# Attention: the loads that stack K and Q are issued by GpSimd in place of SyncE

## The chip, the core and the metric

The kernel runs on one core of a Trainium2 chip. Its engines are TensorE (PE in the profile, its weight loads PEld), VectorE (DVE), ScalarE (ACT), GpSimd (POOL) and SyncE (SP), which here only issues transfers. The metric is the device time of one execution in microseconds (us); lower is better.

## The reference, cut to what matters

One step of a two-layer network over 128 context tokens and 1024 latent tokens (1152 together, `T` in the kernel). The first layer is a state-space mixer with pooling. The second, which this study is about, has 8 differential attention heads (two softmaxes over all keys, one subtracted from the other) and 16 windowed heads that share 4 key heads; the kernel works on them two at a time, in 8 window blocks.

```python
def diff_attention(q, k, v, lam):
    ...
        s = jnp.einsum('bhiqd,bhikd->bhiqk', qb, k).astype(jnp.float32) * scale
        p = jax.nn.softmax(s, axis=-1)
        attn = p[:, :, 0] - lam * p[:, :, 1]
        return jnp.einsum('bhqk,bhkv->bhqv', attn.astype(v.dtype), v)
...
def window_sink_attention(q, k, v, k_ctx, v_ctx, sink):
    ...
        s_w = jnp.einsum('bkgqd,bkwd->bkgqw', qb, kw).astype(jnp.float32) * scale
        s_w = jnp.where(valid, s_w, NEG_INF)
        s_c = jnp.einsum('bkgqd,bkld->bkgql', qb, k_ctx).astype(jnp.float32) * scale
        logits = jnp.concatenate([s_c, s_w, jnp.broadcast_to(sk, s_c.shape[:-1] + (1,))], axis=-1)
        p = jax.nn.softmax(logits, axis=-1).astype(v.dtype)
```

## The kernel before

Every float32 operand of a matmul is split into a float16 high part and a float16 remainder, and products are summed from the parts.

The second layer runs in two stages. The **differential stage** (lines 1473 to 1490) goes over 8 heads, numbered 0 to 7. The **window stage** (lines 1494 to 1509) goes over 8 pairs of window heads, numbered here 8 to 15 after the keys of their Q projections. Each head or pair goes over 9 query blocks of 128 rows, b = 0 to 8. For each block PE forms the scores S from Q and K (line 1288, in the window stage lines 1367 and 1370), DVE and ACT make the softmax, ACT writes the high part of the probabilities into the tile `phl` (line 1304 or 1389), POOL subtracts and writes the remainder (line 1305 or 1390, called the **split** below), SP transposes `phl` by a DMA into the tile `PT` (line 1233), and PE multiplies `PT` by V (line 1321 or 1407). That last product, called PV below, is put off: the PV of block b runs on PE three blocks later, so the PV of block 5 runs at the very end of a pair and those of blocks 6 to 8 in the next.

While a head is worked on, PE also makes the next head's projections, piece by piece between the score matmuls (the `Filler`). `qk_block` (line 1158) makes one K or Q: after the matmuls the result is rotated, with POOL doing the two last steps of each of three pieces (lines 1180 and 1181, on the tiles `sw` and `q`), then ACT writes the high half of `qhl` (line 1187) and POOL the remainder (line 1188). Four transfers then stack the halves of `qhl` from partitions 0 to 63 and 64 to 127 into the tile `K` or `Q` (lines 1193 and 1198): one for each of two matrices `m` and two halves `x`. There are 10 such K and 16 such Q, so 40 and 64 transfers, all issued by SP. The first S of a head or pair needs them all.

Engines take their instructions in order. PE's order is written out by hand (`manual_schedule`), those of the other engines come from a scheduler. SP issues all transfers of the attention in one queue: weights, transposes, K and Q loads, outputs. A transfer that still waits for its input holds up what stands behind it.

Of the kernel before, what the change touches and what calls it, by code (L numbers as in the profile page):

```python
# [22 lines left out]
T = TC + TL  # L23
# [197 lines left out]
class Builder:  # L221
# [936 lines left out]
    def qk_block(self, key, src, hs, cache=None, kout=None, scale=1.0, pre=None):  # L1158

        nc = self.nc  # L1160
        q = self.tl(self.rot, [P, TK], F32, "q32", 2)
        n = T if cache is None else TK
        if cache is not None:
            nc.sync.dma_start(q[:, T:TK], cache)

        def evac(ps, c0, c1):
            raw = self.tl(self.rot, [P, 384], F32, "raw", 2)
            o = TC if c0 == 0 else 0
            nc.scalar.activation(raw[:, o:], ps[:, o:], AF.Copy, scale=scale)
            if c0 == 0:  # L1170
                nc.scalar.activation(q[:, :TC], ps[:, :TC], AF.Copy, scale=IWS * scale)
            a, b = c0 + o - TC, c1 - TC

            if pre is None:
                nc.vector.scalar_tensor_tensor(q[:, c0 + o:c1], ps[:, o:], scale, self.cosT[:, a:b], ALU.mult, ALU.mult)  # L1175
            else:
                nc.vector.tensor_tensor(q[:, c0 + o:c1], raw[:, o:], self.cosT[:, a:b], ALU.mult)
            sw = self.tl(self.rot, [P, 384], F32, "sw", 2)
            nc.vector.stream_shuffle(sw[:, o:], raw[:, o:], [(i + 16) % 32 for i in range(32)])  # L1179
            nc.gpsimd.tensor_tensor(sw[:, o:], sw[:, o:], self.sinT[:, a:b], ALU.mult)  # L1180
            nc.gpsimd.tensor_tensor(q[:, c0 + o:c1], q[:, c0 + o:c1], sw[:, o:], ALU.add)

        yield from self.g_proj(src, hs, evac, pre)
        if kout is not None:
            nc.sync.dma_start(kout, q[:, :TC])
        hl = self.tl(self.rot, [P, 2, TK], F16, "qhl", 2)
        nc.scalar.activation(hl[:, 0, :n], q[:, :n], AF.Copy)
        nc.gpsimd.tensor_tensor(hl[:, 1, :n], q[:, :n], hl[:, 0, :n], ALU.subtract)
        if cache is not None:
            d = self.wt([P, 2, TK], F16, tag="K", bufs=2)  # L1190
            for m in range(2):
                for x in range(2):
                    nc.sync.dma_start(d[x * 64:x * 64 + 64, m], hl[m * 64:m * 64 + 64, x])
        else:
            d = self.wt([P, 2, 2, T], F16, tag="Q", bufs=2)
            for m in range(2):
                for x in range(2):
                    nc.sync.dma_start(d[x * 64:x * 64 + 64, m], hl[m * 64:m * 64 + 64, :, :T])
        self.R[key] = d

    def v_block(self, key, src, hs, vout):
# [450 lines left out]
```

## Time and profile before

| | us |
|---|---|
| median of 3 runs | 2256.24 (2253.14 to 2256.71) |
| the profiled execution, its time | 2259.94 |
| the profiled execution, its span from first to last instruction | 2258.0 |
| PE busy in the span | 2025.2 (90%) |
| DVE busy | 1470.4 (65%) |
| ACT busy | 1223.2 (54%) |
| POOL busy | 1060.9 (47%) |

The 1.9 us between the profiled execution's time and its span lie before the first and after the last instruction. The profile's page gives, for each group of instructions, the engine, the operation, the tile written and the tiles read, the number, the busy time and the idle time of the engine just before them with what ended it. The timeline has one row for each instruction: start in us from the span's start, duration in us, engine, line, operation, tiles, shapes, and in brackets the engine's idle time before it with the releaser. SPq rows are the issues of SP: their duration is that of the issue, not of the transfer. A busy share is an average over stages, so the rows below are taken from the stages in which the changed transfers stand.

### The profile page before, as it was taken

The page shows a single profiled execution, that of the slowest core. Times are in us where ns is not written, and L with a number is a line of the kernel's source. Part 1 is how long each engine was busy: PE and PEld are TensorE (multiplying, and loading weights), DVE is VectorE, ACT ScalarE, POOL GpSimd, SP SyncE. Part 2 cuts the span into 40 slices and gives each one's busy share as a digit, 9 for nine tenths or more (in the row PEclk, how much of TensorE's full clock was granted, in tenths as well). Part 3 has the DMA queues.
Part 4 walks back from the last instruction along what each step waited for, and adds up shares of the span by engine and source line. Part 5 has one row for each costly group of instructions (what it writes and reads, how often), then busy time and mean ns, then how long its engine had stood idle before and what let it go on. Part 6 is the DMA issues. An engine that isn't in the chain of part 4 may idle for free.

```text
span 2258.0 us, 49764 instructions
## 1 busy us (share of the span) xinstructions
PE 2025.2 (90%) x20258; PEld 1433.6 (63%) x20258; DVE 1470.4 (65%) x2722; ACT 1223.2 (54%) x2891; POOL 1060.9 (47%) x997
## 2 busy tenths in 40 slices
PE   5997788887989999998998999999988998998997
PEld 2654475564556655665776776776666777785566
DVE  5878988789586445575677677767765545451334
ACT  5575666566463312344655655665567867782321
POOL 1378677876675200044345345445446655661001
PEclk8998898998999999999999999999999999999999
DMA  7221513224557622035454554555456968899312
GB/s 281 72 79 48 152 58 102 75 94 122 183 202 217 164 99 88 31 132 118 95 122 108 117 123 113 112 126 115 109 123 134 175 146 160 163 176 210 139 47 84
DMA packets 435125, 283.10 MB, mean 125 GB/s; under 512 B 374448, under 2 KB 385232, under 8 KB 434896
## 3 DMA queue, kind: packets, MB, share of 16 engines
q1 hardware_dynamic: 433920, 279.34, 49.9%
q8 instruction: 158, 2.59, 0.5%
q10 hardware_dynamic: 976, 0.58, 0.1%
q14 instruction: 71, 0.58, 0.1%
HBM read 133.38 MB, written 29.05 MB: 72 GB/s over the span
## 4 chain that ended last, share of the span: by engine, by line
PE 42%; DVE 20%; POOL 10%; ACT 9%; issue 6%; DMA 5%; SPq 2%; POOLq 0%; ACTq 0%; DVEq 0%
PE psmm L329 8%; PE psmm L330 8%; PE psmm L331 8%; DVE sms L1290 3%; PE psS L1288 3%; DVE whl L323 3%; PE psm L329 2%; PE psm L330 2%; PE psm L331 2%; DVE p L1303 2%; DMA Q<-qhl 2%; ACT p L1380 1%; ACT p L1292 1%; DVE E L801 1%; PE psss L331 1%
## 5 line engine op out<-in xcount | busy, mean ns | idle before, releaser
L329 PE MATMUL psmm<-h,whl 128*128 128x384 f16 (+1 forms) x1104 | 370.2, 336 | 21.3 <-DVE q L1175 14.7
L330 PE MATMUL psmm<-h,whl 128*128 128x384 f16 (+1 forms) x1104 | 369.1, 335 | 2.3 <-DVE h L506 1.7
L331 PE MATMUL psmm<-h,whl 128*128 128x384 f16 (+1 forms) x1104 | 369.0, 335 | 0.0
L329 PE MATMUL psmm<-whl,h 128*128 128x128 f16 x1920 | 334.0, 220 | 10.1 <-DVE V L1211 10.1
L330 PE MATMUL psmm<-whl,h 128*128 128x128 f16 x1920 | 333.7, 220 | 0.0
L331 PE MATMUL psmm<-whl,h 128*128 128x128 f16 x1920 | 333.6, 220 | 0.0
L330 PEld LDWEIGHTS <-whl 128*128 128x128 f16 x2256 | 225.5, 100 | 167.9 <-issue 47.2
L331 PEld LDWEIGHTS <-whl 128*128 128x128 f16 x2256 | 225.2, 100 | 157.1 <-issue 18.9
L329 PEld LDWEIGHTS <-whl 128*128 128x128 f16 x2256 | 226.3, 100 | 147.3 <-issue 23.3
L1305 POOL TENSOR_TENSOR phl<-p,phl 128x1152 f16<-128x1152 f32 (+1 forms) x72 | 155.9, 2169 | 218.5 <-ACT phl L1304 218.5
L330 PEld LDWEIGHTS <-h 128*128 128x128 f16 x2520 | 246.7, 98 | 12.6 <-issue 10.8
L329 PEld LDWEIGHTS <-h 128*128 128x128 f16 x2520 | 246.8, 99 | 4.3 <-issue 2.6
L331 PEld LDWEIGHTS <-h 128*128 128x128 f16 x2520 | 246.6, 98 | 0.0
L323 DVE SCALAR_TENSOR_TENSOR whl<-w,whl 128x512 f16<-128x512 f32 x248 | 196.5, 811 | 67.0 <-ACT whl L322 66.0
L1290 DVE TENSOR_REDUCE sms<-psS 128x1 f32<-128x1152 f32 (+1 forms) x136 | 176.5, 1298 | 67.0 <-PE psS L1288 66.2
L1390 POOL TENSOR_TENSOR phl<-p,phl 128x1024 f16<-128x1024 f32 (+2 forms) x72 | 135.1, 1876 | 106.8 <-ACT phl L1389 85.8
L322 ACT ACTIVATE whl<-w 128x512 f16<-128x512 f32 x248 | 140.1, 609 | 78.2 <-PE psmm L331 42.2
L1288 PE MATMUL psS<-K,Q 128*128 128x512 f16 (+1 forms) x800 | 153.2, 328 | 25.1 <-DVE p L1303 19.3
L1180 POOL TENSOR_TENSOR sw<-sw,sin 128x384 f32<-128x384 f32 (+1 forms) x78 | 85.8, 1101 | 150.6 <-DVE sw L1179 127.2
L503 POOL TENSOR_TENSOR h<-mt,h 128x384 f16<-128x384 f32 (+2 forms) x32 | 28.9, 913 | 250.0 <-ACT h L502 250.0
L1288 PEld LDWEIGHTS <-Q 128*128 128x128 f16 x800 | 73.5, 99 | 94.2 <-DVE p L1303 21.9
L1292 ACT ACTIVATE psS<-psS,sms 128x1152 f32<-128x1152 f32 (+1 forms) x72 | 79.1, 1098 | 89.4 <-DVE sms L1290 88.9
(396 smaller groups left out, 5864.7 us busy)
## 6 DMA issues: line engine op xcount, KB each, us to landing
w<-in_wod SPq DMA_DIRECT2D x52, 512.0 KB, 4.0
w<-in_wev SPq DMA_DIRECT2D x40, 512.0 KB, 4.1
E<-csrow SPq DMA_DIRECT2D x36, 512.0 KB, 4.0
Q<-qhl SPq DMA_DIRECT2D x64, 288.0 KB, 4.3
go_dr<-gl SPq DMA_DIRECT2D x15, 576.0 KB, 3.9
wada<-in_w_ada SPq DMA_DIRECT2D x32, 256.0 KB, 5.8
o<-in_w_ada SPq DMA_DIRECT2D x16, 512.0 KB, 5.8
xT<-in_w_ada SPq DMA_DIRECT2D x16, 512.0 KB, 6.1
```

The source lines that it names most:

```text
L322: nc.scalar.activation(hl[:, 0, a:e], w[:, a:e], AF.Copy if scale is None else AF.Identity, scale=sc)
L323: nc.vector.scalar_tensor_tensor(hl[:, 1, a:e], w[:, a:e], sc, hl[:, 0, a:e], ALU.mult, ALU.subtract)
L329: mm(out, ah, bh, start=start, stop=False)
L330: mm(out, ah, bl, start=False, stop=False)
L331: mm(out, al, bh, start=False, stop=stop)
L1180: nc.gpsimd.tensor_tensor(sw[:, o:], sw[:, o:], self.sinT[:, a:b], ALU.mult)
L1288: nc.tensor.matmul(sv[:, i, c0:c1], q[:, m, x, qs], k[:, m, o + c0:o + c1], start=x == 0, stop=x == 1)
L1290: nc.vector.tensor_reduce(out=sm[:, ms[0]:ms[-1] + 1], in_=sv, axis=AX.X, op=ALU.max, negate=True)
L1292: nc.scalar.activation(sv[:, i] if m else e, sv[:, i], AF.Exp, bias=sm[:, m:m + 1], accum_out=sm[:, 4 + m:5 + m])
L1303: nc.vector.scalar_tensor_tensor(p[0], p[1], sm[:, 2:3], p[0], ALU.mult, ALU.add)
L1305: nc.gpsimd.tensor_tensor(phl[:, w:2 * w], p[0], phl[:, :w], ALU.subtract)
L1390: nc.gpsimd.tensor_tensor(phl[:, 2 * w:4 * w], p, phl[:, :2 * w], ALU.subtract)
```

## The change

The two `dma_start` calls that stack K and Q go from SP's queue to POOL's. Nothing else in the source changes: sizes, tiles and waits for data are the same.

```diff
@@ -1190,12 +1190,12 @@
             d = self.wt([P, 2, TK], F16, tag="K", bufs=2)
             for m in range(2):
                 for x in range(2):
-                    nc.sync.dma_start(d[x * 64:x * 64 + 64, m], hl[m * 64:m * 64 + 64, x])
+                    nc.gpsimd.dma_start(d[x * 64:x * 64 + 64, m], hl[m * 64:m * 64 + 64, x])
         else:
             d = self.wt([P, 2, 2, T], F16, tag="Q", bufs=2)
             for m in range(2):
                 for x in range(2):
-                    nc.sync.dma_start(d[x * 64:x * 64 + 64, m], hl[m * 64:m * 64 + 64, :, :T])
+                    nc.gpsimd.dma_start(d[x * 64:x * 64 + 64, m], hl[m * 64:m * 64 + 64, :, :T])
         self.R[key] = d
```

The orders of PE, DVE and ACT stay word for word the same. POOL's and SP's change. On POOL in the window stage, at the Q of the second pair (L1188 is the last step of Q's split, L1390 the splits of the probabilities of blocks 5 and 6):

```order
 L1390 TENSOR_TENSOR phl_21686<-p_21598,phl_21686 128x1024
 L1188 TENSOR_TENSOR qhl_21552<-q_2258_21263,qhl_21552 128x1152
+L1198 DMA Q_21555<-qhl_21552 64x2x1152 x4
 L1390 TENSOR_TENSOR phl_21789<-p_21692,phl_21789 128x1024
 L1390 TENSOR_TENSOR phl_21892<-p_21795,phl_21892 128x1024
```

All four loads now stand in one piece between the end of Q's split and the split of block 5. The same place on SP, where L1233 are the transposes of blocks 4, 5, 6 and 7 and L312 is a load of weights:

```order
 L312 DMA w_2470_23138<-in_wod 128x1024
 L1233 DMA_TRANSPOSE PT_21689<-phl_21686 128x16x128
-L1198 DMA Q_21555<-qhl_21552 64x2x1152 x2
 L1233 DMA_TRANSPOSE PT_21792<-phl_21789 128x16x128
-L1198 DMA Q_21555<-qhl_21552 64x2x1152
 L1233 DMA_TRANSPOSE PT_21895<-phl_21892 128x16x128
-L1198 DMA Q_21555<-qhl_21552 64x2x1152
 L1233 DMA_TRANSPOSE PT_21995<-phl_21992 128x16x128
```

The transposes now stand next to one another; before, the third and fourth load stood behind one and two of them. On POOL in the differential stage, at the K of head 2 (L1180 and L1181 rotate the first piece of the next Q, L1305 is a split of probabilities):

```order
 L1188 TENSOR_TENSOR qhl_13289<-q_1502_13053,qhl_13289 128x1280
+L1193 DMA K_13292<-qhl_13289 64x1280 x2
+L1180 TENSOR_TENSOR sw_13368<-sw_13368,sin_11482 128x256
+L1193 DMA K_13292<-qhl_13289 64x1280
+L1181 TENSOR_TENSOR q_1533_13297<-q_1533_13297,sw_13368 128x256
+L1193 DMA K_13292<-qhl_13289 64x1280
 L1305 TENSOR_TENSOR phl_13336<-p_13204,phl_13336 128x1152
-L1180 TENSOR_TENSOR sw_13368<-sw_13368,sin_11482 128x256
-L1181 TENSOR_TENSOR q_1533_13297<-q_1533_13297,sw_13368 128x256
```

Here the four K loads stand ahead of the split of probabilities, and the first piece's rotation has also gone ahead of it.

## The prediction

> **What bounds the kernel now.** I read the stages by window first, then what PE waits for in each, then the timeline of POOL, SP and PE where K and Q are loaded. Columns of the first view: the stretch, its length, busy time of PE, PEld, DVE, ACT and POOL with instructions, granted clock, DMA share, GB/s.
>
> ```profile
> 1025.00:1677.00 652.00, 601.01 (x6806) 457.38 (x6806) 467.66 (x697) 386.89 (x758) 301.92 (x185) 0.97 0.52 114
> 1677.00:2050.00 373.00, 332.99 (x4787) 272.11 (x4786) 192.68 (x596) 272.61 (x772) 221.41 (x138) 0.95 0.83 160
> ```
>
> The first row is the differential stage, the second the window stage. PE is the bound of both (601 of 652 us, 333 of 373 us), and POOL is busy 46% and 59% of the time. Whatever this change does, it does through PE's waits. From the view of waits (waiter, releaser, us in total, times, longest), the two rows on L1288 over the differential stage, the three others over the window stage:
>
> ```profile
> PE psS L1288 <- DVE p L1303: 19.3, 11, 5.1
> PE psS L1288 <- DMA Q<-qhl: 5.7, 2, 3.9
> ...
> PE psS L1367 <- DMA Q<-qhl: 15.8, 6, 5.8
> PE pssm L1407 <- DMA PT<-phl: 5.0, 3, 2.6
> PE pss L1407 <- DMA PT<-phl: 4.6, 2, 2.7
> ```
>
> PE waits 15.8 us for Q at six of the pairs, and 5.7 us for the first head's Q. It never waits for K. It waits another 9.6 us for `PT`, the transposed probabilities, in the window stage. So the most that earlier Q loads can give is 15.8 + 5.7 = 21.5 us (1%), and the 40 K loads can give nothing.
>
> **The price of an issue.** No transfer is issued by POOL in this trace, so the price c of one issue there is bounded by rows:
>
> ```profile
> L1198 SPq DMA_DIRECT2D Q<-qhl x64: 591/613/1592, 1017.2 to 1996.6; - x64
> DMA to landing us min/median/max: 3.3/4.3/7.2
> ...
> L1305 POOL TENSOR_TENSOR phl<-p,phl x72: 426/2373/2827, 1030.5 to 1683.3; 128x1152 f16<-128x1152 f32 x64, 128x128 f16<-128x128 f32 x8
> ```
>
> On SP a Q load takes 613 ns (median) and at most 1592 ns to issue, and lands 4.3 us after the start of its issue. These are my ends, c = 0.61 and 1.59 us. POOL's shortest instruction of this stage (426 ns) shows what starting anything on that engine costs; 0.61 + 0.43 gives c = 1.0 us, which I take for K and Q loads alike. It is nearer to the lower end, as most rows are: half of SP's issues of this load take between 591 and 613 ns. (The Trainium skill, "DMA: Bandwidth & Descriptors", section Specifications, gives a first byte after about 1 us for a transfer from GpSimd and about 0.6 us for one from SP; an estimate from that page is 0.6 + 0.4 = 1.0 us for c, and with it the sum would be the same. No run here shows it.)
>
> **The window stage, pair 8.** SP, then POOL, then PE:
>
> ```profile
> 1713.83 1.30 SPq L1198 DMA_DIRECT2D Q<-qhl  x2
> 1715.92 4.07 SPq L1233 DMA_TRANSPOSE PT<-phl  x1
> 1720.04 0.60 SPq L1198 DMA_DIRECT2D Q<-qhl  x1
> 1724.26 0.60 SPq L1198 DMA_DIRECT2D Q<-qhl  x1
> ...
> 1711.43 2.38 POOL L1188 TENSOR_TENSOR qhl<-q,qhl 128x1152 f16<-128x1152 f32 x1
> 1713.76 2.13 POOL L1390 TENSOR_TENSOR phl<-p,phl 128x1024 f16<-128x1024 f32 x1
> ...
> 1721.41 0.20 PE L1407 MATMUL pssm<-V,PT 128*128 128x64 f16 x1 [0.55 <-DMA PT<-phl]
> 1728.14 0.37 PE L1367 MATMUL psS<-K,Q 128*128 128x128 f16 x2 [5.75 <-DMA Q<-qhl]
> ```
>
> Q's split ends at 1711.43 + 2.38 = 1713.81. Two loads go at once, but the third and fourth stand behind transposes and the last goes out at 1724.26; PE sits from 1722.39 to 1728.14 for it. Issued on POOL, the four would be out at 1713.81 + 4c = 1717.8, and the last, started at 1716.8, would land at 1721.1. That wait is gone.
>
> What is late next is the split of block 5 (the L1390 row), now behind four issues. It would end at 1713.81 + 4c + 2.13. Its transpose then lands how much later? Before, it was issued at 1715.92 and PE was released at 1721.41, 5.5 us; the median of all transposes of this stage is 4.3:
>
> ```profile
> DMA to landing us min/median/max: 2.5/4.3/8.6
> ```
>
> Before, Q loads ran beside this transpose; afterwards they are mostly through. I take 4.9, half way. So PV of block 5 starts at 1713.81 + 4.0 + 2.16 + 4.9 = 1724.9 and not 1721.41; S follows 0.98 us later, as before (1722.39 − 1721.41), at 1725.85 and not 1728.14: **2.3 us gained of the 5.75**. One wait takes the place of the other.
>
> **The other pairs** go the same way, with the Q split's end plus 4c + 2.16 + 4.9 + 0.98 against the S of before. Pair 9 and pair 14, the last with this pattern (6 pairs: 8, 9, 10, 12, 13, 14):
>
> ```profile
> 1755.40 2.38 POOL L1188 TENSOR_TENSOR qhl<-q,qhl 128x1152 f16<-128x1152 f32 x1
> 1760.22 3.69 SPq L1233 DMA_TRANSPOSE PT<-phl  x1
> 1767.17 0.20 PE L1407 MATMUL pss<-V,PT 128*128 128x64 f16 x1 [1.93 <-DMA PT<-phl]
> 1769.03 0.35 PE L1367 MATMUL psS<-K,Q 128*128 128x128 f16 x2 [0.88 <-ACT sms L1382]
> ...
> 1986.62 2.38 POOL L1188 TENSOR_TENSOR qhl<-q,qhl 128x1152 f16<-128x1152 f32 x1
> 1998.32 0.20 PE L1407 MATMUL pssm<-V,PT 128*128 128x64 f16 x1 [1.85 <-DMA PT<-phl]
> 2001.24 0.37 PE L1367 MATMUL psS<-K,Q 128*128 128x128 f16 x2 [1.94 <-DMA Q<-qhl]
> ```
>
> Pair 9: 1757.78 + 4.0 + 2.16 + 4.9 + 0.98 = 1769.8 against 1769.03, 0.8 us lost, since there PE hardly waited for Q. Pair 14: 2001.0 against 2001.24, 0.2 gained. From the same kind of rows, pair 10 loses 0.35, pair 12 loses 0.7, pair 13 gains 1.0. The six sum to **1.6 us gained**. Pair 11 has other work between (its block 5 is long done); its Q can land between 1.7 us sooner and 0.5 us later than before, I take 0.5 gained. Stage: 2.1 us gained. Each 0.1 us in c moves this by 6 x 0.4 = 2.4 us, which makes c the number that decides.
>
> **Head 0**, before the differential stage proper, where K and Q follow one another on POOL:
>
> ```profile
> 1003.13 2.61 POOL L1188 TENSOR_TENSOR qhl<-q,qhl 128x1280 f16<-128x1280 f32 x1 [1.38 <-ACT qhl L1187]
> 1007.20 0.73 POOL L1180 TENSOR_TENSOR sw<-sw,sin 128x256 f32<-128x256 f32 x1 [1.46 <-DVE sw L1179]
> 1014.84 2.37 POOL L1188 TENSOR_TENSOR qhl<-q,qhl 128x1152 f16<-128x1152 f32 x1 [1.27 <-ACT qhl L1187]
> ...
> 1025.19 0.39 PE L1288 MATMUL psS<-K,Q 128*128 128x128 f16 x2 [3.88 <-DMA Q<-qhl]
> 1027.44 0.37 PE L1288 MATMUL psS<-K,Q 128*128 128x128 f16 x2 [1.86 <-DMA Q<-qhl]
> ```
>
> K's four loads take 4.0 us of POOL, and 1.46 of them fall into its idle time, so Q's split ends 2.5 us later, at 1019.7. With three issues, one rotation step (0.73) and the fourth issue started at 1023.4, Q's last landing is 1023.4 + 4.3 to 1023.4 + 7.2, that is 1027.7 to 1030.6 against 1027.44. I take **1.7 us lost**.
>
> **The other heads.** 8 issues a head add 8 us to POOL's 301.92 / 8 = 38 of 652 / 8 = 82. At K the four issues and the first piece's rotation (2 x 0.73) come ahead of a split, here of block 2 of head 2:
>
> ```profile
> 1214.28 2.36 POOL L1305 TENSOR_TENSOR phl<-p,phl 128x1152 f16<-128x1152 f32 x1
> 1222.99 2.01 POOL L1180 TENSOR_TENSOR sw<-sw,sin 128x384 f32<-128x384 f32 x1 [4.35 <-DVE sw L1179]
> ...
> 1230.87 0.22 PE L1321 MATMUL psS<-V,PT 128*128 128x128 f16 x1 [0.34 <-ACT og L1330]
> ```
>
> The split would end at 1214.3 + 4.0 + 1.46 + 2.36 = 1222.1, before POOL's next work at 1222.99, and its transpose would land by 1226.8 (4.6 us, the median of all transposes, quoted below); PE needs it at 1230.87. Cost nothing, and PE never waited for K itself. If POOL were not idle there, the rotations behind would be late by up to the 5.5 us. At the Q of the same turn the cover is thinner:
>
> ```profile
> 1239.19 2.36 POOL L1305 TENSOR_TENSOR phl<-p,phl 128x1152 f16<-128x1152 f32 x1
> ...
> 1251.21 0.22 PE L1321 MATMUL psS<-V,PT 128*128 128x128 f16 x1
> ```
>
> The split moves from 1239.19 to 1243.2, its transpose follows at 1245.6, and with 4.6 us to land `PT` is there at 1250.2; PE needs it at 1251.21. Covered by 1.0 us; from c = 1.25 on each of 7 heads pays 4 us for each further us. On SP 64 x 0.61 + 40 x 0.57 = 62 us of issuing go away, and the waits of SP for `qhl`; but PE waits for none of SP's other transfers in the differential stage, and for the transposes of the window stage it is counted above.
>
> ```profile
> L1193 SPq DMA_DIRECT2D K<-qhl x40: 461/567/808, 1003.1 to 1836.1; - x40
> PT<-phl SPq DMA_TRANSPOSE x144, 4.6
> ```
>
> **The sum:** −2.1 + 1.7 + 0 = −0.4 us: no change. Made on the profiled execution (span 2258.0, time 2259.94, which is 3.7 above the median of the runs); carried to the median, 2256.24 − 0.4 = 2256 us.
>
> **The rivals.**
>
> *Issues are as cheap on POOL as on SP* (c = 0.61). For it: the transfers are the same and POOL is idle 41% of the window stage. Against: SP does nothing but issue. The six pairs then gain 1.6 + 2.4 x 3.9 = 11, pair 11 another 1, and head 0 gains 1 instead of losing: 13 us, 2243 us.
>
> *DVE holds POOL up while it issues.* This one ends slower. POOL's rotation of a 128x384 piece takes 1.00 us in the row at 1742.86 and 1354 ns as the mean of the differential stage, where it runs beside DVE work:
>
> ```profile
> 1742.86 1.00 POOL L1180 TENSOR_TENSOR sw<-sw,sin 128x384 f32<-128x384 f32 x1 [2.75 <-DVE sms L1386]
> ...
> L1180 POOL TENSOR_TENSOR sw<-sw,sin 128x384 f32<-128x384 f32 x31 | 42.0, 1354 | 95.8 <-DVE sw L1179 92.6 <-DVE rqa L377 3.2
> ```
>
> If issues are stretched as much, c = 1.35: pairs 1.6 − 8.4 = −6.8, pair 11 −0.9, head 0 −4.5, and the seven heads with 5.4 against 5.0 us of cover 0.4 x 7 = −2.9. Together 15 us slower, 2271 us; it decides from about c = 1.14, where the sum passes 4.5 us. (The Trainium skill, "SBUF — State Buffer", section "SBUF: two separate sides", speaks against the change: descriptors of a GpSimd transfer are written by GpSimd through ports that it shares with VectorE, and while VectorE runs an instruction that takes both port pairs none can be written. The stretched rotations agree that the two engines hold each other up; no run here shows it for an issue.)
>
> *Transposes land later.* In pair 9 the transpose of block 5 took 1767.17 − 1760.22 = 6.95 us with Q loads beside it. If loads from a second queue keep doing that, the landing is 6.9 and not 4.9 us: 6 x 2.0 = 12 us lost, some 12 us slower, 2268 us. Against: on POOL all four are out before that transpose starts.
>
> **How the numbers follow.** About 0.2% (4.5 us) is what a measurement of this kernel tells from no change. My forecast, no change, has a chance of 0.37 (c between about 0.87 and 1.14). Cheap issues: 0.28. DVE's hold: 0.25, late transposes: 0.10. So faster 0.28, same 0.37, slower 0.35. The range reaches from the cheap case, 2243, past 2271 to what c = 1.4 gives (2275); the end c = 1.59 (pairs −12.5, pair 11 −1.9, head 0 −6.4, heads 1.4 x 7 = −9.7, some 2287 us) is left out with the tail. The likeliest case's own range is 2252 to 2261.
>
> **What would show it.** In the changed kernel's profile: the issues of L1198 and L1193 on POOL's queue, with their duration, which should be near 1.0 us; PE's waits for Q in the window stage down from 15.8 us to under 4, and those for `PT` up from 9.6 to about 20; the split of block 5 starting about 4 us after Q's split ends; no wait for `PT` at L1321. The prediction fails if an issue on POOL takes clearly less than 0.87 or more than 1.14 us, or if the loads, issued together, take longer than 7 us to land.

## The result: 1.3% slower, and the profile after

| | before | after |
|---|---|---|
| median of the runs, us | 2256.47 (4 runs) | 2286.10 (4 runs, 2284.50 to 2290.24) |
| ratio to before | | 1.0129, 95% interval 1.0112 to 1.0146 |
| the profiled execution's time, us | 2259.94 | 2284.72 |
| its span, us | 2258.0 | 2282.9 |

The changed kernel is some 30 us slower; between the two profiled executions it is 24.8 us, and between their spans 24.9. The forecast was no change, and the time lies outside its range. Two executions among the experiments below were slower than all others by far, 2910 us in one_k and 5247 us in k_ts, and the medians leave them out. First the number on which the forecast rested, the issues (ns, min/median/max, first and last start in us), in the changed kernel's answer for the two lines:

```profile
L1198 POOL DMA_DIRECT2D Q<-qhl x64: 587/594/636, 1020.2 to 2012.0; - x64
...
L1193 POOL DMA_DIRECT2D K<-qhl x40: 523/534/727, 1007.3 to 1855.8; - x40
```

An issue costs POOL 0.59 and 0.53 us: the cheap end, at which the prediction's sum gave 2243 us. So the price of an issue was not what decided. Where does the time go? PE's order is the same in both kernels, so the same matmul can be looked up in both timelines. The first S of head 1 and the first S of the window stage, before:

```profile
1102.56 0.63 PE L1288 MATMUL psS<-K,Q 128*128 128x128 f16 x4
...
1678.87 0.38 PE L1367 MATMUL psS<-K,Q 128*128 128x128 f16 x4 [1.77 <-ACT og L1330]
```

and after:

```profile
1104.75 0.63 PE L1288 MATMUL psS<-K,Q 128*128 128x128 f16 x4
...
1698.42 0.38 PE L1367 MATMUL psS<-K,Q 128*128 128x128 f16 x4 [1.77 <-ACT og L1330]
```

PE is 2.2 us behind at head 1 and 19.5 us behind at the window stage: **17.4 us are lost in heads 1 to 7**, 1.9 to 3.0 in each, where the prediction had nothing. The last matmul of the program is 19.1 us behind, so the window stage and what follows change by −0.4. The span is 24.9 us longer, so **5.8 us come behind the last matmul**. What PE waits for over 990 to 2080 us (us in total, times, longest), first in the kernel before, whose stretch here is longer than that of the prediction's rows and so has more waits for `PT`:

```profile
PE pssm L1407 <- DMA PT<-phl: 9.4, 4, 4.4
PE pss L1407 <- DMA PT<-phl: 8.8, 5, 2.7
```

```profile
PE psS L1288 <- DVE p L1303: 34.3, 11, 7.6
PE pssm L1407 <- DMA PT<-phl: 20.8, 6, 4.4
...
PE pss L1407 <- DMA PT<-phl: 12.2, 4, 4.9
...
PE psS L1367 <- DMA Q<-qhl: 3.0, 1, 3.0
PE psS L1321 <- DMA PT<-phl: 2.7, 4, 1.2
```

The waits for Q in the window stage fall by 12.8 us (15.8 to 3.0) and those for `PT` at L1407 rise by 14.8 (18.2 to 33.0): that stage exchanges one wait for another, as forecast, and comes out even. What was not forecast is the first row: in the heads PE waits 15.0 us more for DVE (19.3 before).

Not all of these 15.0 us are lost, since PE's waits for V (L1211) fall from 10.8 to 3.3 us. Over heads 1 to 7 PE's idle time grows by 9.3 us and its busy time from 532.0 to 540.1, at a granted clock of 0.95 in place of 0.98. A lower clock alone does not make a head longer here: head 2 takes 83.00 us at 1.00 in the kernel before and 82.97 at 0.98 in its repeat, and heads 3, 4 and 5 of the run dummy_k below take 84.14, 84.10 and 84.09 at 0.96, 0.98 and 0.96.

**Why DVE is late.** Head 3, at the K of the next head. DVE works on the previous head's output there: a reciprocal root of nine numbers a partition (L374 to L379), the scaling of `og` (L1249), and behind that the reduce (L1290) on which the softmax waits. POOL, then DVE, before:

```profile
1297.27 2.36 POOL L1305 TENSOR_TENSOR phl<-p,phl 128x1152 f16<-128x1152 f32 x1
...
1297.37 2.29 DVE L377 TENSOR_TENSOR rqa<-rqy,oss 128x9 f32<-128x9 f32 x1
...
1302.31 1.36 DVE L1249 TENSOR_TENSOR og<-og,orr 128x1152 f32<-128x1152 f32 x1
```

and after:

```profile
1304.37 1.09 POOL L1193 DMA_DIRECT2D K<-qhl  x2
1305.48 0.74 POOL L1180 TENSOR_TENSOR sw<-sw,sin 128x256 f32<-128x256 f32 x1
1306.15 0.56 POOL L1193 DMA_DIRECT2D K<-qhl  x1
1306.72 0.73 POOL L1181 TENSOR_TENSOR q<-q,sw 128x256 f32<-128x256 f32 x1
1307.39 0.53 POOL L1193 DMA_DIRECT2D K<-qhl  x1
1307.94 2.38 POOL L1305 TENSOR_TENSOR phl<-p,phl 128x1152 f16<-128x1152 f32 x1
...
1304.49 0.17 DVE L377 TENSOR_TENSOR rqa<-rqy,oss 128x9 f32<-128x9 f32 x1
...
1306.49 3.87 DVE L377 TENSOR_TENSOR rqa<-rqy,oss 128x9 f32<-128x9 f32 x1
...
1311.01 1.36 DVE L1249 TENSOR_TENSOR og<-og,orr 128x1152 f32<-128x1152 f32 x1
```

A DVE operation on nine columns, which takes 0.17 us two microseconds earlier in the changed kernel, is held until POOL's split ends: to 1299.66 before (the split ends at 1299.63), to 1310.36 after (1310.32). It was already held in the kernel before; now POOL goes through a rotation, an issue and the split without a gap, and the hold is 3.87 us in place of 2.29. DVE takes its instructions in order, so L1249 starts at 1311.01 and not at 1302.31 + 7.12 (what PE was behind at the start of this head): 1.58 us late.

**The end.** The drain of POOL at the end of the program (ns, min/median/max of three), before and after:

```profile
L1642 POOLq DRAIN  x3: 34/77/1572, 2252.9 to 2257.7; - x3
```

```profile
L1642 POOLq DRAIN  x3: 34/102/10095, 2272.1 to 2282.7; - x3
```

and POOL's last operation in the timeline after:

```profile
2272.10 1.48 POOL L1540 TENSOR_TENSOR yo<-yo,rb 128x384 f32<-128x384 f32 x1 [6.52 <-DVE rb L379]
```

It ends at 2273.58, yet the drain, which starts at 2272.1, takes 10.10 us and ends at 2282.2. Before, it ended with the operation. The drain is 8.5 us longer; other work (the last outputs land) hides 2.7 of it, and 5.8 are left.

### The profile page after: what moved, and what is told of

Same layout as the page of the kernel before. It is cut to its first block, busy times and chain, and to the rows that moved or that the text cites. A ratio compares the mean times of both kernels' runs of the same rounds, so it can differ in the third digit from the quotient of the medians.

```text
span 2282.9 us, 49801 instructions
## 1 busy us (share of the span) xinstructions
PE 2026.5 (89%) x20258; PEld 1440.6 (63%) x20258; DVE 1480.9 (65%) x2722; ACT 1222.0 (54%) x2891; POOL 1119.7 (49%) x1101
## 4 chain that ended last, share of the span: by engine, by line
PE 40%; DVE 22%; POOL 12%; issue 6%; DMA 6%; ACT 6%; SPq 1%; POOLq 0%; ACTq 0%; DVEq 0%
PE psmm L329 7%; PE psmm L331 7%; PE psmm L330 7%; DMA PT<-phl 4%; DVE sms L1290 3%; DVE whl L323 3%; PE psS L1288 2%; PE psm L329 2%; PE psm L331 2%; PE psm L330 2%; DVE p L1303 2%; DVE rqa L377 1%; DVE E L801 1%; POOL qhl L1188 1%; PE psss L331 1%
## 5 line engine op out<-in xcount | busy, mean ns | idle before, releaser
L329 PE MATMUL psmm<-whl,h 128*128 128x128 f16 x1920 | 342.3, 223 | 14.7 <-DVE q L1175 12.9
L330 PE MATMUL psmm<-whl,h 128*128 128x128 f16 x1920 | 342.0, 223 | 0.0
L331 PE MATMUL psmm<-whl,h 128*128 128x128 f16 x1920 | 341.6, 223 | 0.0
L330 PEld LDWEIGHTS <-h 128*128 128x128 f16 x2520 | 249.8, 100 | 17.9 <-issue 16.7
L1305 POOL TENSOR_TENSOR phl<-p,phl 128x1152 f16<-128x1152 f32 (+1 forms) x72 | 155.6, 2165 | 200.0 <-ACT phl L1304 199.5
L329 PEld LDWEIGHTS <-h 128*128 128x128 f16 x2520 | 250.0, 100 | 4.3 <-issue 2.8
L331 PEld LDWEIGHTS <-h 128*128 128x128 f16 x2520 | 249.7, 100 | 0.0
L1290 DVE TENSOR_REDUCE sms<-psS 128x1 f32<-128x1152 f32 (+1 forms) x136 | 176.5, 1298 | 71.1 <-PE psS L1288 70.3
L1390 POOL TENSOR_TENSOR phl<-p,phl 128x1024 f16<-128x1024 f32 (+2 forms) x72 | 135.1, 1881 | 87.7 <-ACT phl L1389 84.0
L1180 POOL TENSOR_TENSOR sw<-sw,sin 128x384 f32<-128x384 f32 (+1 forms) x78 | 86.0, 1103 | 141.5 <-DVE sw L1179 119.3
```

What stands on the lines that cost most here:

```text
L329: mm(out, ah, bh, start=start, stop=False)
L330: mm(out, ah, bl, start=False, stop=False)
L331: mm(out, al, bh, start=False, stop=stop)
L1290: nc.vector.tensor_reduce(out=sm[:, ms[0]:ms[-1] + 1], in_=sv, axis=AX.X, op=ALU.max, negate=True)
L1305: nc.gpsimd.tensor_tensor(phl[:, w:2 * w], p[0], phl[:, :w], ALU.subtract)
L1390: nc.gpsimd.tensor_tensor(phl[:, 2 * w:4 * w], p, phl[:, :2 * w], ALU.subtract)
```

## The experiments

All times are medians beside runs of the kernel before on the same chip (2255.0 to 2255.9 us, and 2256.5 for the change). The stage columns are from one profile each: us that PE falls behind the first profile of the kernel before over heads 1 to 7, then from the first S of the window stage to the last matmul, then what the span adds behind the last matmul, and the length of POOL's drain.

| run | time − before | ratio, 95% interval | heads 1–7 | window on | end | drain |
|---|---|---|---|---|---|---|
| the change | +29.6 | 1.0112–1.0146 | 17.4 | −0.4 | 5.8 | 10.10 |
| k_only | +12.1 | 1.0039–1.0068 | 12.8 | −4.4 | 0.6 | 4.86 |
| q_only | +10.6 | 1.0025–1.0058 | 4.0 | 4.8 | 2.5 | 6.83 |
| one_k | +2.3 | 1.0000–1.0023 | 0.2 | −1.1 | −0.2 | 1.92 |
| split_first | +64.1 | 1.0255–1.0295 | 31.5 | 19.5 | 5.8 | 10.09 |
| dummy_q | +14.5 | 1.0055–1.0079 | −0.2 | 7.9 | 2.5 | 6.83 |
| dummy_k | +14.2 | 1.0044–1.0072 | 9.4 | −0.8 | 0.6 | 4.86 |
| k_dve2 | +9.4 | 1.0031–1.0057 | 9.0 | −1.0 | 0.6 | 4.86 |
| before_dve2 | +8.5 | 1.0022–1.0045 | 8.4 | −6.5 | 0.3 | 1.57 |
| q_win_half | +6.3 | 1.0009–1.0036 | 0.7 | 4.3 | 0.1 | 2.91 |
| q_win_act | +10.7 | 1.0030–1.0060 | 0.5 | 4.5 | 0.0 | 1.57 |
| k_ts | +11.4 | 1.0035–1.0067 | 11.5 | −1.4 | 0.6 | 4.86 |
| before_again | | | 0.2 | −0.4 | 0.0 | 1.57 |

The repeat of the unchanged kernel shows that the heads repeat to 0.2 us; it also stood 3.5 us earlier already at head 1. Of the 2.2 us that the change is behind there, 1.7 were there at 987 us, ahead of its first changed load (1007.3), and are the spread of executions. The window column is less firm: the runs that leave the loads of Q alone spread from −6.5 to −0.4 (one_k, before_dve2 and before_again change nothing in that stage at all, and give −1.1, −6.5 and −0.4).

**K alone and Q alone on POOL.**

```diff
-nc.sync.dma_start(d[x * 64:x * 64 + 64, m], hl[m * 64:m * 64 + 64, x])
+nc.gpsimd.dma_start(d[x * 64:x * 64 + 64, m], hl[m * 64:m * 64 + 64, x])
```

> Only the 40 loads of K are issued by POOL; the 64 of Q stay on SP. In the changed kernel the matmuls of PE fall behind those of the kernel before by 17.5 us over heads 1 to 7 (2.1 to 3.0 a head), and about 1.8 of each head's share is there before its Q loads are issued, the rest (0.4 to 1.2, PE waiting for PT of block 4) after. Theory A (the split of block 2, moved behind the K issues, holds up VectorE's small operations of the previous head and through them the reduces): heads 1 to 7 lose 11 to 14 us here, the window stage about 0, the end of the program 5 to 6, so 2272 to 2277 us. Theory B (what costs is the Q loads, whose packets lie in their own queue beside the transposes): heads lose under 3 us here, so 2262 to 2265 us. In both, POOL's last drain is near 10 us if that cost comes with any load issued by POOL.

In the other run only the line of Q is changed.

> Only the 64 loads of Q are issued by POOL; the 40 of K stay on SP. Theory A: heads 1 to 7 lose 3 to 6 us (the waits for PT of block 4), the window stage about what it nets in the changed kernel (+2.6), the end of the program 5 to 6: 2267 to 2271 us. Theory B: heads lose 14 us or more: 2277 to 2283 us.

The heads lose 12.8 us with K alone and 4.0 with Q alone: theory A's shares, and B is out. The times are lower than expected, mostly since the end costs 0.6 and 2.5 us and not 5 to 6: POOL's drain is 4.86 and 6.83 us.

**Four loads on POOL.**

```diff
-nc.sync.dma_start(d[x * 64:x * 64 + 64, m], hl[m * 64:m * 64 + 64, x])
+(nc.gpsimd if key == ("k", 0) else nc.sync).dma_start(d[x * 64:x * 64 + 64, m], hl[m * 64:m * 64 + 64, x])
```

> Only head 0's four K loads, some 1230 us ahead of the end, are issued by POOL. If POOL's last drain (10.10 us in the changed kernel, 1.57 before) is the price of having issued any load from POOL, it is near 10 us here too, and the time is 5 to 7 us above the kernel before: 2262 to 2264 us. If it grows with the number of loads (104 there, 4 here), it is under 2.5 us here and the time is within 1.5 us of the kernel before.

The drain is 1.92 us, so it grows with the number of loads. With 0, 4, 16, 40, 64 and 104 loads it is 1.57, 1.92, 2.91, 4.86, 6.83 and 10.10 us: 0.08 us a load throughout. It is the same to 0.01 us whether the 64 or 40 loads carry Q and K or the few bytes of the runs below. The time is nearer to the kernel before than a drain of 10 us would leave it, though 2.3 us above, where at most 1.5 were expected.

**The split ahead of the other issues.**

```diff
-            nc.gpsimd.tensor_tensor(phl[:, w:2 * w], p[0], phl[:, :w], ALU.subtract)
+            with self.tc.high_priority(): nc.gpsimd.tensor_tensor(phl[:, w:2 * w], p[0], phl[:, :w], ALU.subtract)
```

and the same at L1390.

> All 104 loads stay on POOL, but the split of each block gets high priority, so that it stands behind one issue and not behind two to four and the rotation. Theory A (the place of the split): most of the 17.5 us of heads 1 to 7 goes, under 4 left; the window stage's late transposes go in part; the end's 5.8 us stays: 2262 to 2268 us. Theory B (the loads' own queue beside the transposes, or the issue time itself): heads still lose 12 us or more: 2276 us or above.

The run is 64 us slower. Theory A missed by far. Theory B's bound (2276 us or above) is met, but nothing in it led to 64 us. The place of the split is not the only thing that counts. Head 4 at the Q of the next head, in the changed kernel and then in this run:

```profile
1416.71 2.39 POOL L1198 DMA_DIRECT2D Q<-qhl  x4 [0.30 <-POOL qhl L1188]
1419.10 2.39 POOL L1305 TENSOR_TENSOR phl<-p,phl 128x1152 f16<-128x1152 f32 x1
...
1421.52 8.69 SPq L1233 DMA_TRANSPOSE PT<-phl  x2
...
1429.84 0.23 PE L1321 MATMUL psS<-V,PT 128*128 128x128 f16 x1 [1.19 <-DMA PT<-phl]
```

```profile
1421.13 0.63 POOL L1198 DMA_DIRECT2D Q<-qhl  x1 [0.30 <-POOL qhl L1188]
1421.78 2.38 POOL L1305 TENSOR_TENSOR phl<-p,phl 128x1152 f16<-128x1152 f32 x1
1424.10 1.78 POOL L1198 DMA_DIRECT2D Q<-qhl  x3
...
1424.19 4.34 SPq L1233 DMA_TRANSPOSE PT<-phl  x1
...
1435.21 0.23 PE L1321 MATMUL psS<-V,PT 128*128 128x128 f16 x1 [2.24 <-DMA PT<-phl]
```

The three loads now go out together with the transpose of the same block, and PE gets `PT` 11.0 us after its issue, where it was 8.3 in the changed kernel (the issues of two transposes stand in one row there). The trace tells the landing of about a third of the transposes. For those of 1100 to 1720 us, nearly all of them of the heads, the answer for L1233 gives, in the kernel before, the changed one and this one:

```profile
DMA to landing us min/median/max: 2.3/4.6/6.2
```

```profile
DMA to landing us min/median/max: 2.3/4.6/7.8
```

```profile
DMA to landing us min/median/max: 2.3/5.5/11.1
```

On SP the loads and the transposes stood in one queue: block 4's landed after 5.3 to 5.4 us with two Q loads ahead of it and two behind, which went out some 4 us after it. With the four loads in POOL's queue it lands after 7.1 to 7.8, and after 11.0 to 11.1 with three of them issued beside it. (The Trainium skill, "DMA: Bandwidth & Descriptors", section "Queues, rings and completion order", has each transfer engine go round the queues that have work for it, a packet at a time. The 11.0 us fit that: a transpose shares the engines with what another queue holds.) Whether the 7.1 to 7.8 come from the second queue, or from four loads ahead of the transpose in place of two, no run here tells apart. Two rival readings of Q's loss were left, the bytes beside the transpose and POOL's time, and the next run tells them apart.

**POOL's time without the bytes.** Q is loaded by SP as before, and POOL issues small loads in Q's places.

```diff
+            z = self.wt([P, 2, 2, 16], F16, tag="zz", bufs=1)
...
                     nc.sync.dma_start(d[x * 64:x * 64 + 64, m], hl[m * 64:m * 64 + 64, :, :T])
+                    nc.gpsimd.dma_start(z[x * 64:x * 64 + 64, m], hl[m * 64:m * 64 + 64, :, :16])
```

> Q is loaded by SP as before; POOL issues 64 further loads at the places where it issued the Q loads in the run with Q alone on POOL, each of 128 rows of 32 bytes into a spare tile. POOL's order is that run's, SP's order that of the kernel before. Theory C (what Q costs is bytes in flight beside the transposes, in a queue of their own): heads 1 to 7 lose under 1.5 us and block 4's transpose lands near 5.4 us as before, so 2255 to 2259 us, with 2.5 to 3.5 us of it at the program's end. Theory D (POOL's issue time and the place of the split): heads lose 4 us or more as with Q on POOL, so 2260 us or more.

The small loads in the groups of instructions (busy us, mean ns), and PE's waits:

```profile
L1200 POOL DMA_DIRECT2D zz<-qhl x64 | 38.0, 601 | 4.7 <-POOL qhl L1188 4.7
```

```profile
PE psS L1369 <- DMA Q<-qhl: 18.7, 7, 5.3
PE pssm L1409 <- DMA PT<-phl: 14.3, 6, 3.5
...
PE pss L1409 <- DMA PT<-phl: 6.7, 4, 2.2
```

(The lines are two further on than before.) The small loads take as long to issue as Q's, 601 ns, and stand at the same places, but the heads lose nothing (−0.2), where Q on POOL lost 4.0: **in the heads Q costs by its own bytes, taken from SP's queue and set beside the transposes**, not by POOL's time, and the split's move by 2.4 us is covered. The time was missed all the same, since the window stage loses 7.9 us, with the waits for Q kept (18.7 against 15.8) and those for `PT` at 21.0 (18.2 before). That points to POOL's time costing something there too, but it is one profile. The same with 40 small loads in K's places:

> K is loaded by SP as before; POOL issues 40 further loads of 64 rows of 32 bytes at the places where it issued the K loads in the run with K alone on POOL. Theory A (POOL's work ahead of the split of block 2 holds VectorE up): heads 1 to 7 lose 8 to 12 us as with K alone, so 2264 to 2268 us. Theory C (K's bytes in their own queue): under 3 us lost in the heads, 2256 to 2259 us.

The heads lose 9.4 of K's 12.8 us: **K costs mostly by POOL's time**, not by its bytes. That time is the four issues and the rotation that goes ahead with them; the two are not separated. The run's time, 2270.1 us, is 2 us above what theory A gave.

**The split of block 2 on DVE**, with K on POOL and then in the kernel before.

```diff
-            nc.gpsimd.tensor_tensor(phl[:, w:2 * w], p[0], phl[:, :w], ALU.subtract)
+            (nc.vector if b == 2 and h else nc.gpsimd).tensor_tensor(phl[:, w:2 * w], p[0], phl[:, :w], ALU.subtract)
```

> K on POOL, Q on SP, and the split of block 2 of heads 1 to 7 on VectorE, so that POOL has no split of 2.4 us behind the K issues that could hold VectorE's two-operand operations. Theory A: VectorE's L377 operations are no longer held for over 2.5 us, and most of the 10 us that K cost in heads 1 to 7 is gone: at most 4 us lost there, 2255 to 2261 us, less what 1.4 us of VectorE costs a head. Theory C: the loss in the heads stays, 2264 us or more.

> The kernel before, K and Q on SP, with the split of block 2 of heads 1 to 7 on VectorE. In the kernel before L377 is already held for 2.29 us by that split. If such a hold lies on the path, this gains 0.5 to 1.5 us a head, 2245 to 2252 us; if the next wait ends no earlier, it is within 3 us of the kernel before.

No small operation takes over 1.1 us in heads 1 to 7 any more, except one of 1.39 in head 1 and one of 1.43 in head 7, but both kernels lose, 9.0 and 8.4 us: the edit moves DVE's order, and PE then waits more for ACT (4.8 us before), here in the second of the two:

```profile
PE psS L1321 <- ACT og L1330: 17.8, 11, 2.2
```

Neither expectation held: k_dve2's 2265.3 us lies where theory C put it, but the kernel without any load on POOL loses nearly as much. What can be read is the difference of the two: with this split on DVE, K on POOL costs the heads 0.6 us, against 12.8 with the split on POOL.

**Another kind of operation in DVE's place.** K is on POOL. The nine small operations of the reciprocal root have one operand and copy, so the kernel leaves its refinement out.

```diff
+                for o, i in ((a, y), (a, a), (out if it == 2 else y, a)):
+                    nc.vector.tensor_scalar(o, i, 1.0, 0.0, ALU.mult, ALU.add)
...
```

> K on POOL, Q on SP, and the three refinement steps of the reciprocal root in the heads' output (L377 to L379, nine small operations with two operands in SBUF) replaced by nine of one operand that only copy, so that the refinement is left out. The orders of POOL and of VectorE are those of the run with K alone on POOL. Theory A1 (VectorE's two-operand operations are held until POOL's split ends, and the reduces behind them come late): no operation of 128x9 takes over 1.5 us, and heads 1 to 7 lose at most 5 us of the 12.8 that they lost there: 2250 to 2260 us. Theory A2 (the split of block 2 and its transpose come late, whatever VectorE does): they still lose 11 us or more: 2265 to 2269 us. If the one-operand operations are held as well, the run tells nothing apart.

```profile
1298.75 3.86 DVE L379 TENSOR_SCALAR rqa<-rqy 128x9 f32<-128x9 f32 x1
...
1300.19 2.38 POOL L1309 TENSOR_TENSOR phl<-p,phl 128x1152 f16<-128x1152 f32 x1
```

The copies are held just as long, so this run tells A1 and A2 (a late split and late transpose, whatever DVE does) not apart. But the runs together do. Head 3 in each; "late" is the start less that in the kernel before, less what PE was behind at the head's first S:

| run | longest hold of a small operation | split of block 2 late | L1249 late | S of block 6 late |
|---|---|---|---|---|
| before_again | 2.29 | 0.00 | 0.01 | 0.00 |
| q_only | 2.29 | 0.00 | 0.01 | 0.01 |
| split_first | 2.88 | 0.58 | 1.06 | 1.06 |
| dummy_k | 3.32 | 3.50 | 1.12 | 1.16 |
| k_only | 3.87 | 3.54 | 1.56 | 1.55 |
| k_ts | 3.86 | 3.53 | 1.57 | 1.56 |
| the change | 3.87 | 3.55 | 1.57 | 1.74 |

PE's loss follows DVE's lateness one to one, and not the split's: a split 0.58 or 3.50 late costs the same 1.1 us (in the change the last 0.17 us come behind L1249). In split_first a second hold of 1.04 us comes behind the first. That settles K for A1. (The Trainium skill, "SBUF — State Buffer", section "Who interferes with whom", says that VectorE and GpSimd share a pair of ports as an exclusive lock, and that a VectorE operation with two inputs in SBUF contends for it and a one-input `tensor_scalar` may. The traces agree: both kinds are held here, up to 3.87 us. They differ in one thing: the page has the pair taken for one whole instruction, and here the hold goes on through several of POOL's.)

**Half of the window stage's Q on another queue**, POOL's and then ACT's.

```diff
-nc.sync.dma_start(d[x * 64:x * 64 + 64, m], hl[m * 64:m * 64 + 64, :, :T])
+(nc.gpsimd if key[1] > 7 and m else nc.sync).dma_start(d[x * 64:x * 64 + 64, m], hl[m * 64:m * 64 + 64, :, :T])
```

> Only the loads m=1 of the eight window Q (16 loads) are issued by POOL; all else is as before. In the kernel before two of a pair's four loads go out ahead of the transpose of block 5 and two behind it; here the latter two go out beside it from POOL. If POOL's issue time is what costs in the window stage (the run with 64 small loads lost 9.9 us there with 32 issues of 0.6 us in it), half of it costs about 5, and the waits of PE for Q (15.8 us) fall by 6 to 10: 2250 to 2255 us. If bytes beside the transpose cost more than they gain, PE's wait for PT of block 5 grows to over 3 us a pair, and it is 2256 to 2262 us. The end of the program is under 0.5 us later.

> The same 16 loads, issued by ACT. No POOL time, no split moved behind an issue, no longer drain of POOL, but the same bytes beside the transposes and 1.2 us of ACT a pair. If POOL's issue time was what cost, this is 2 to 6 us better than the run with these loads on POOL; if the bytes were, it is within 2 us of it.

Waits of PE in the run with POOL, then in the run with ACT:

```profile
PE pssm L1407 <- DMA PT<-phl: 19.5, 5, 4.5
...
PE pss L1407 <- DMA PT<-phl: 13.5, 5, 4.7
```

```profile
PE pssm L1407 <- DMA PT<-phl: 15.2, 6, 3.8
...
PE psS L1367 <- ACT p L1380: 12.1, 11, 1.5
PE pss L1407 <- DMA PT<-phl: 9.9, 5, 4.0
```

With two loads a pair on POOL the waits for Q at L1367 are gone from the view, which has one wait of 3.9 us there without a releaser, and those for `PT` are 33.0 us, as with all four. With ACT they are 25.1, and PE waits 9.7 us more for ACT's exponentials (2.4 before). Both are slower than the kernel before, by 6.3 and 10.7 us: just past the bytes' end of what was expected for POOL, and for ACT 4 us worse than that, which neither reading expected. How much of the 33.0 us is bytes and how much the two issues ahead of the split isn't separated here. No version tried beats the kernel before.

> The kernel before, once more, to see how far two profiles of one kernel agree: the matmuls of PE at the starts of the heads and pairs within 3 us of the first profile's, the losses over heads 1 to 7 within 1 us, over the window stage within 3 us.

It agrees in the heads and the window stage; the starts of the heads differ by up to 3.9 us, 0.9 more than expected.

## Why the prediction was wrong, step by step

- **"c the number that decides": failed.** It was taken as 1.0 us and is 0.53 to 0.59. By the prediction's own sum that gave 13 us faster, and the kernel is 30 slower. What decided lay outside the sum.
- **The other heads, K: "Cost nothing": the step that failed most.** It looked at POOL's idle time and at when `PT` is needed, and with K alone on POOL no loss came by either. It did not look at DVE, which stands still until POOL's stretch of work ends. The row for it was there, in the kernel before: a nine-column operation of 2.29 us, ending with POOL's split. The step was put at nothing and measured 12.8 us with K alone.
- **The other heads, Q: "Covered by 1.0 us": failed.** POOL was quicker than assumed and the cover held for POOL's time (dummy_q: no loss). But the 4.6 us for the transpose to land is the median of all. Block 4's took 5.3 to 5.4 already in the kernel before, and takes 7.1 to 7.8 beside the loads of POOL's queue. That costs 0.3 to 1.4 us in six of the heads in the change, 4.0 in all with Q alone.
- **The window stage: the exchange was right, its sizes were not.** Waits for Q below 4 us: 3.0. Waits for `PT` "up from 9.6 to about 20" (those rows ended at 2030 us; over the whole stage 18.2): 33.0. In pair 8:

```profile
1730.96 2.38 POOL L1188 TENSOR_TENSOR qhl<-q,qhl 128x1152 f16<-128x1152 f32 x1
1733.63 2.37 POOL L1198 DMA_DIRECT2D Q<-qhl  x4 [0.30 <-POOL qhl L1188]
1736.01 4.24 POOL L1390 TENSOR_TENSOR phl<-p,phl 128x1024 f16<-128x1024 f32 x2
...
1744.43 0.23 PE L1407 MATMUL pssm<-V,PT 128*128 128x64 f16 x1 [4.04 <-DMA PT<-phl]
```

  The split of block 5 ends half way through the row of two, at 1738.13, and PE is released 6.3 us later, not 4.9. The rival "transposes land later" named this and put it at 6.9; it was right that they land later, and its argument against itself, that all four loads are out before the transpose starts, did not help: they are issued, but have not landed (a Q load lands 5.2 us after its issue in the median, and the four issues end only 2.1 us ahead of the split's end). The small issues and the late landings cancel, −0.4 us where −2.1 was forecast; with the spread of that column the two are not told apart.
- **Head 0: 1.7 us lost was too much.** PE is 1.7 us behind ahead of these loads and 2.2 at head 1, so they cost some 0.5, little more than the starts move in the repeat.
- **The end of the program was left out**, since no row of the kernel before shows that a load issued by POOL has a price there: 5.8 us.
- The rival "DVE holds POOL up" had the two engines right and the direction wrong: Q's issues take 587 to 636 ns and only the longest of K's comes to 727, its loads land after 2.6 us (median) in both kernels, and it is POOL that holds DVE.

The parts add up to 2.2 + 17.4 − 0.4 + 5.8 = 25.0 us between the two profiles (24.9 before rounding). The medians differ by 29.6: the profiled execution before is 3.5 us above its median and the one after 1.4 below. In which stage these other 4.7 us lie stays open.

## What to carry to other kernels

When work is added to an engine, look not only at what waits for its results but also at operations of other engines that already end exactly when one of its own ends: they can be held by it, and here each moment without a gap made the hold longer. Loads and transposes in one queue keep their order; a second queue took the loads' wait away here and let them run into the transposes. A price of the moved instruction itself, right or wrong, says little before these two have been looked at.

## What the runs showed of the hardware

- POOL's drain at the end of the program grows by 0.08 us for each load that POOL has issued, whether it carries 2 or 288 KB and although the loads landed long before: 1.57 us with none, 10.10 with 104.
- A DVE operation of 0.17 us was held for 3.87 us, through three POOL instructions without a gap between them, one of which was an issue of 0.53 us that computes nothing. A copy with one operand was held like a product of two.
- An issue on POOL costs about the same as on SP (0.59 against 0.61 us for Q) and does not depend on the bytes (0.60 us for 4 KB).
